# Moving the tiles of a matrix-product kernel to whole 2 KB addresses

## The chip, the cores and the metric

One core of a Trainium2 chip runs the kernel. The metric is the device time of one execution in microseconds. TensorE (PE) makes the matrix products, VectorE (DVE), ScalarE (ACT) and GpSimd (POOL) the rest; SyncE (SP) issues most DMAs. SBUF is the on-chip memory: 128 partitions, each a row of bytes, and an address here is a byte offset that is the same in all partitions. A tile of 128 rows by 512 fp32 elements takes 2048 bytes (2 KB) of every partition.

## The reference

One layer over 512 frames of width 2048: RMS norm, one input projection, two mixing branches (a gated recurrence and a differential attention), a projection of each branch, a gated merge, an output projection and the residual:

```python
h = rms_norm(x, norm_w[l])
proj = jnp.einsum('btd,dn->btn', h, w_in[l])
...
ya = hgrn2_mixer(a_q, a_f, a_i, lb_all[l], a_out_norm[l]).astype(x.dtype) * jax.nn.silu(a_g)
yb = diff_attention(b_q, b_k, b_v, b_q_norm[l], b_k_norm[l], b_lambda[l],
                    b_subln[l], lambda_init).astype(x.dtype) * jax.nn.silu(b_g)
ya = jnp.einsum('btw,wd->btd', ya, w_branch_a[l])
yb = jnp.einsum('btw,wd->btd', yb, w_branch_b[l])
mixed = jax.nn.sigmoid(gate_a) * ya + jax.nn.sigmoid(gate_b) * yb
x = x + jnp.einsum('btd,de->bte', mixed, w_out[l])
```

All of it is fp32. The kernel computes the large products with operands split in two float32r parts, a high and a low one, and three products of the parts (high by high, high by low, low by high).

## The kernel before

Nearly all the work is in `gemm` (line 148), which makes 512 columns of a projection. It goes over the contraction in blocks of 256 rows (`KC` = 2 times 128). For each block SP loads a `raw` tile (two rows of 512 elements, 4 KB, line 155), ACT rounds it to `whi` (line 167), DVE subtracts to get `wlo` (line 168), and PE makes 24 products: 4 output tiles by 2 contraction rows by 3 part pairs, all at line 183, all with a stationary operand of 128 by 128 elements (512 bytes of a partition, the slice `js` at 512 times j bytes into its tile) and a moving operand of 128 by 512 (2048 bytes). Every product loads its own stationary operand.

Three kinds of product stand at line 183, and the text names them by what moves:

- kind G: the normed input moves (`h_hi`, `h_lo`; tiles hh and hl), the weights (`whi`, `wlo`) are stationary. These are the first projections of branch A and the merge gates: 12 calls of 192 products, 2304 in all.
- kind W: the weights move, the normed input is stationary. These are the second projections of branch A (4 calls) and the projections of the 8 heads of branch B: 12 calls, 2304 products.
- kind S: the branch outputs or the merged rows move (tiles named s, from `split`), the weights are stationary. Branch projections (8 calls of 96) and the output projection (4 calls of 192): 1536 products.

The order of work is set by a scheduler that simulates the program; the code gives it priorities (`tc.high_priority`). The order in which `hybrid_block` calls things: branch A's four pairs of heads, each `proj_a` (a G call, then a W call) and two `mix_a`; the first two heads of branch B (`proj_b`, then `mix_b`); `merge` of branch A, in which G calls for the gates alternate with S calls; the other six heads of B; `merge` of branch B; the output projection. The small work of a mixer (products of 128 to 512 columns such as those of lines 294, 489 and 518, masks, exponentials) is interleaved with the products of the next call of `gemm`. I call a stretch of time in which that happens a mixer stage.

Where tiles lie is set by the pools (lines 69 to 73) in the order in which they are opened, each tile a multiple of 32 bytes. The first pool starts at address 16512, which is 128 past a whole 2 KB (16384). The pool `const` comes first, and in it the table `sm` (line 86, 292 elements, 1168 bytes), the small constants, then the 32 tiles of `h_hi` and `h_lo` (lines 107 and 108). In the built program the tiles lie, past the last whole 2 KB, at

| tiles | before | after |
|---|---|---|
| hh, hl (32 tiles of 2 KB) | 352 | 0 |
| raw (2), whi (3), wlo (3), 4 KB each | 1184 | 0 |
| slots s0 to s48 (2 KB each) | 1184 | 0 |
| qm (two of 3 KB, operand of line 294) | 288, 1312 | 0, 1024 |
| ident, the moving operand of the transposes | 1312 | 0 |

Since each large tile is a whole number of 2 KB long, all tiles of a row of this table have the same offset. A stationary slice adds 0, 512, 1024 or 1536 to it.

Of the kernel before, what the change touches and what calls it, by code (L numbers as in the profile page):

```python
# [10 lines left out]
F32 = mybir.dt.float32  # L11
F32R = mybir.dt.float32r
# [5 lines left out]
P = 128  # L18
T = 512
NT = T // P  # L20
D = 2048
NK = D // P
# [8 lines left out]
NSLOT = 49  # L31
PRIO = 3000
LEVELS = (2, 8, 32)


C_NW = 0
# [6 lines left out]
N_SMALL = C_LAM + 4 * QK  # L43
# [20 lines left out]
def hybrid_block(ctx: ExitStack, tc: tile.TileContext, xT, w_in, w_a, w_b, w_out,  # L64
# [1 line left out]
    nc = tc.nc  # L66
    MUL, ADD, SUB = ALU.mult, ALU.add, ALU.subtract

    const = ctx.enter_context(tc.tile_pool(name="const", bufs=1))
    wpool = ctx.enter_context(tc.tile_pool(name="wpool", bufs=3))  # L70
    spool = ctx.enter_context(tc.tile_pool(name="spool", bufs=1))
    small = ctx.enter_context(tc.tile_pool(name="small", bufs=4))
    qmp = ctx.enter_context(tc.tile_pool(name="qmp", bufs=2))
    ps_acc = ctx.enter_context(tc.tile_pool(name="ps_acc", bufs=4, space=bass.MemoryType.PSUM))
    ps_mix = ctx.enter_context(tc.tile_pool(name="ps_mix", bufs=4, space=bass.MemoryType.PSUM))

# [6 lines left out]
        return ps_mix.tile([P, T], F32, name="mix", tag="mix")  # L83


    sm = const.tile([P, N_SMALL], F32, name="sm")
    nc.scalar.dma_start(out=sm[:, 0:C_LAM], in_=smalls[:, 0:C_LAM])
    ident = const.tile([P, P], F32, name="ident")
    make_identity(nc, ident)
# [14 lines left out]
            slots.put(mi)  # L104


    h_hi = [const.tile([P, T], F32R, name=f"hh{k}") for k in range(NK)]
    h_lo = [const.tile([P, T], F32R, name=f"hl{k}") for k in range(NK)]
    xacc_s = slots.get()
    xacc = xacc_s[0]  # L110
    rstd_t = const.tile([P, NT], F32, name="rstd_t")
# [155 lines left out]
    def mix_a(head, q, sp, sn, vg, hh, dest):  # L267
# [19 lines left out]
        def scores(level, kt, qm):  # L287
            c = (1,) + LEVELS
            c = c[level]
            for half in range(2):  # L290
                ps = mix_tile()
                for i in range(2):
                    tt = half * 2 + i
                    nc.tensor.matmul(ps[:, i * 192:(i + 1) * 192], lhsT=kt[:, tt * P:(tt + 1) * P],  # L294
                                     rhs=qm[:, tt * 192:(tt + 1) * 192], start=True, stop=True)
                out = sc[:, half * 2:half * 2 + 2, :].rearrange("p i t -> p (i t)")
                mk = masks[:, level, :]
                if level == 0:
                    parts = ((0, 2, 0), (1, 2, 2))
                    w = 3  # L300
                    n = 2
                else:
                    parts = ((c, 4 * c, 0), (2 * c, 4 * c, 3 * c), (3 * c, 4 * c, 5 * c))
                    w = 6 * c
                    n = 4 * c
                ov = out.rearrange("p (g m) -> p g m", m=n)
                dv = ps[:, 0:384].rearrange("p (g m) -> p g m", m=w)
                kv = mk.rearrange("p (g m) -> p g m", m=w)
                for a, b, s0 in parts:
                    nc.vector.copy_predicated(out=ov[:, :, a:b], mask=kv[:, :, s0:s0 + b - a],  # L310
                                              data=dv[:, :, s0:s0 + b - a])
# [15 lines left out]

        for level, c in enumerate(LEVELS):
            G = T // (4 * c)
# [327 lines left out]
def _consts():  # L657
# [8 lines left out]
    for i in range(2):  # L666
        for g in range(P // 2):
# [3 lines left out]
            masks[:, 0, c0 + 2] = s == 2 * g  # L671
        for lv, c in enumerate(LEVELS):
            for g in range(P // (4 * c)):
# [46 lines left out]
```

## Time and profile before

| what | before |
|---|---|
| median of 3 runs | 1561.41 us (1559.88 to 1562.16) |
| the profiled execution's own time | 1564.39 us |
| its span, first to last instruction | 1562.6 us |
| mean granted TensorE clock | 0.997 of full speed |
| PE busy | 1546.7 us (99%) |
| DVE busy, ACT busy, POOL busy | 742.8 us (48%), 589.6 us (38%), 113.2 us (7%) |
| mean traffic | 100 GB/s |

The profiled execution is 3.0 us above the median and 1.8 us above its own span. A row of the chain of waits gives a start, a length and what ran: since the products follow each other without idle time, the length divided by the count is the step from the start of one product to the start of the next. The mean duration of one product in the tables is longer than this step, because products are pipelined and overlap; the step is what counts for the time.

### The profile page before, as it was taken

To read this page: it belongs to the slowest core of one execution; us is meant where nothing else is said; L and a number is where in the kernel's file an instruction comes from. 1 tells how busy PE (TensorE), PEld (TensorE's weight loads), DVE (VectorE), ACT (ScalarE), POOL (GpSimd) and SP (SyncE) were. 2 spreads that over 40 slices of the span, in tenths; PEclk is the share of its full clock that TensorE was granted. 3 is DMA by queue.
4 is the path that set the end of the run, shared out by engine and by line. 5 is a ranking of instruction groups with operands and counts; after the bars stand their busy time and mean duration, and the time that the engine had idled before them with its cause. 6 is when DMAs were issued, how large, how long until landed. Compare 5 with 4: busy or idle time off the path is not lost.

```text
span 1562.6 us, 18423 instructions
## 1 busy us (share of the span) xinstructions
PE 1546.7 (99%) x7096; PEld 1277.0 (82%) x7096; DVE 742.8 (48%) x1479; ACT 589.6 (38%) x866; POOL 113.2 (7%) x109
## 2 busy tenths in 40 slices
PE   7999999999999999999999999999999999999998
PEld 5888888888888888888888888888888888888887
DVE  8457656575674553322233454545453424442322
ACT  6533633544425552221213455445552222222111
POOL 7000000000011200000001011101100000000000
PEclk9999999999999999999999999999999999999999
DMA  6332222222323233333233333234323333354431
GB/s 213 95 108 68 75 89 77 87 80 68 96 81 97 79 104 92 95 94 96 95 94 102 108 102 100 83 101 103 103 78 94 95 96 95 94 161 148 148 122 68
DMA packets 149400, 155.50 MB, mean 100 GB/s; under 512 B 8192, under 2 KB 107392, under 8 KB 149312
## 3 DMA queue, kind: packets, MB, share of 16 engines
q1 hardware_dynamic: 142944, 143.55, 30.6%
q10 hardware_dynamic: 6288, 10.51, 2.5%
q8 instruction: 56, 0.92, 0.2%
q0 software_dynamic: 80, 0.26, 0.1%
q14 instruction: 32, 0.26, 0.0%
HBM read 143.80 MB, written 4.19 MB: 95 GB/s over the span
## 4 chain that ended last, share of the span: by engine, by line
PE 97%; DVE 1%; issue 1%; SPq 0%; DMA 0%; ACT 0%; DVEq 0%; ACTq 0%
PE acc L183 89%; PE mix L294 3%; PE mix L518 1%; DVE hl L119 1%; PE mix L490 1%; PE mix L489 1%; PE mix L511 1%; PE mix L379 0%; PE mix L453 0%; PE mix L254 0%; DVE wlo L168 0%; PE mix L368 0%; PE mix L382 0%; DMA raw<-in_w_in_dram 0%; SPq L406 0%
## 5 line engine op out<-in xcount | busy, mean ns | idle before, releaser
L168 DVE TENSOR_TENSOR wlo<-raw,whi 128x1024 fp32r<-128x1024 f32 (+1 forms) x257 | 317.2, 1234 | 620.0 <-ACT whi L167 604.1
L167 ACT ACTIVATE whi<-raw 128x1024 fp32r<-128x1024 f32 (+1 forms) x257 | 270.8, 1054 | 717.7 <-PE acc L183 634.8
L183 PE MATMUL acc<-s,whi 128*128 128x512 f32 x1024 | 313.3, 389 | 0.0
L183 PE MATMUL acc<-hh,whi 128*128 128x512 f32 x768 | 306.6, 400 | 5.9 <-ACT whi L167 5.9
L183 PE MATMUL acc<-hh,wlo 128*128 128x512 f32 x768 | 303.2, 400 | 6.0 <-DVE wlo L168 6.0
L183 PE MATMUL acc<-hl,whi 128*128 128x512 f32 x768 | 305.8, 399 | 0.0
L183 PE MATMUL acc<-whi,hh 128*128 128x512 f32 x768 | 303.9, 396 | 0.0
L183 PE MATMUL acc<-wlo,hh 128*128 128x512 f32 x768 | 303.4, 395 | 0.0
L183 PE MATMUL acc<-whi,hl 128*128 128x512 f32 x768 | 301.6, 395 | 0.0
L183 PEld LDWEIGHTS acc<-s,whi 128*128 128x128 f32 x1024 | 192.2, 188 | 40.2
L183 PE MATMUL acc<-s,wlo 128*128 128x512 f32 x512 | 197.1, 389 | 0.0
L183 PEld LDWEIGHTS acc<-hh,wlo 128*128 128x128 f32 x768 | 145.6, 190 | 41.6 <-DVE wlo L168 7.4
L183 PEld LDWEIGHTS acc<-hh,whi 128*128 128x128 f32 x768 | 145.2, 189 | 39.3 <-ACT whi L167 5.9
L183 PEld LDWEIGHTS acc<-hl,whi 128*128 128x128 f32 x768 | 145.2, 189 | 33.7
L183 PEld LDWEIGHTS acc<-whi,hl 128*128 128x128 f32 x768 | 144.5, 188 | 30.3
L183 PEld LDWEIGHTS acc<-wlo,hh 128*128 128x128 f32 x768 | 144.5, 188 | 30.2
L183 PEld LDWEIGHTS acc<-whi,hh 128*128 128x128 f32 x768 | 144.5, 188 | 29.2
L183 PEld LDWEIGHTS acc<-s,wlo 128*128 128x128 f32 x512 | 96.1, 188 | 19.9
L438 POOL TENSOR_TENSOR qr<-qs,mhalf 128x4 f32<-128x4 f32 x32 | 38.8, 1214 | 323.6 <-DVE qs L437 323.6
L310 DVE COPY_PREDICATED s<-s,mix 128x128 f32<-128x128 uint8 (+3 forms) x176 | 52.2, 339 | 14.7 <-PE mix L294 13.6
L294 PE MATMUL mix<-qm,s 128*128 128x192 f32 x256 | 46.9, 326 | 0.0
L495 ACT ACTIVATE s<-s,mn 128x128 f32<-128x128 f32 (+3 forms) x64 | 35.5, 556 | 26.9 <-DVE mn L492 26.9
(137 smaller groups left out, 1094.6 us busy)
## 6 DMA issues: line engine op xcount, KB each, us to landing
raw<-in_w_in_dram SPq DMA_DIRECT2D x240, 256.0 KB, 3.0
raw<-in_w_in_dram SPq DMA_DIRECT2D x64, 512.0 KB, 3.7
raw<-in_w_out_dram SPq DMA_DIRECT2D x32, 512.0 KB, 3.8
raw<-in_w_a_dram SPq DMA_DIRECT2D x16, 512.0 KB, 3.7
raw<-in_w_b_dram SPq DMA_DIRECT2D x16, 512.0 KB, 3.8
s<-s ACTq DMA_DIRECT2D x48, 128.0 KB, 3.9
s<-in_xT_dram SPq DMA_DIRECT2D x16, 256.0 KB, 4.2
raw<-in_w_in_dram SPq DMA_DIRECT2D x32, 128.0 KB, 2.9
```

The costliest lines, as they stand in the source:

```text
L119: nc.vector.scalar_tensor_tensor(out=h_lo[k], in0=x_t, scalar=nw, in1=h_hi[k].bitcast(F32), op0=MUL, op1=SUB)
L167: nc.scalar.activation(out=whi[:, cs, :], in_=raw[:, cs, :], func=AF.Copy)
L168: nc.vector.tensor_tensor(out=wlo[:, cs, :], in0=raw[:, cs, :], in1=whi[:, cs, :].bitcast(F32), op=SUB)
L183: nc.tensor.matmul(accs[j], lhsT=l, rhs=r, start=(k == 0 and n == 0), stop=(k == nk - 1 and n == 2))
L294: nc.tensor.matmul(ps[:, i * 192:(i + 1) * 192], lhsT=kt[:, tt * P:(tt + 1) * P], rhs=qm[:, tt * 192:(tt + 1) * 192], start=True, stop=True)
L310: nc.vector.copy_predicated(out=ov[:, :, a:b], mask=kv[:, :, s0:s0 + b - a], data=dv[:, :, s0:s0 + b - a])
L438: nc.gpsimd.tensor_tensor(out=rr, in0=ss, in1=mhalf[:, 0:4], op=ALU.pow)
L489: nc.tensor.matmul(pc, lhsT=q2[c][0][:, ts], rhs=k2[c][0][:, 0:nm], start=True, stop=False)
L490: nc.tensor.matmul(pc, lhsT=q2[c][0][:, ts], rhs=kl2[c][0][:, 0:nm], start=False, stop=True)
L495: nc.scalar.activation(out=pr[c][0][:, 0:n], in_=pr[c][0][:, 0:n], func=AF.Exp, scale=-1.0, bias=mn[:, e:e + 1], accum_out=z[:, e:e + 1])
L511: nc.tensor.transpose(pt[:, j * P:(j + 1) * P], w[:, j * P:(j + 1) * P], ident)
L518: nc.tensor.matmul(o[:, i * P:(i + 1) * P], lhsT=wTs[i][0][:, j * P:(j + 1) * P], rhs=tiles[j][0][:, 256:384], start=(j == 0), stop=(j == i))
```

## The change

The pools are opened in another order: a new pool `lead` that holds `sm` alone, widened from 292 to 480 elements (1920 bytes, so that 16512 and 1920 end at 18432, which is 9 times 2048), then a new pool `hpool` for `h_hi` and `h_lo`, then `wpool`, `spool` and `qmp`, and only then `const` and `small` with the small tiles. The widened part of `sm` is never written or read.

```diff
@@ -31,6 +31,7 @@
+LEAD = 480
@@ -66,11 +67,14 @@
-    const = ctx.enter_context(tc.tile_pool(name="const", bufs=1))
+
+    lead = ctx.enter_context(tc.tile_pool(name="lead", bufs=1))
+    hpool = ctx.enter_context(tc.tile_pool(name="hpool", bufs=1))
     wpool = ctx.enter_context(tc.tile_pool(name="wpool", bufs=3))
     spool = ctx.enter_context(tc.tile_pool(name="spool", bufs=1))
+    qmp = ctx.enter_context(tc.tile_pool(name="qmp", bufs=2))
+    const = ctx.enter_context(tc.tile_pool(name="const", bufs=1))
     small = ctx.enter_context(tc.tile_pool(name="small", bufs=4))
-    qmp = ctx.enter_context(tc.tile_pool(name="qmp", bufs=2))
@@ -83,7 +87,7 @@
-    sm = const.tile([P, N_SMALL], F32, name="sm")
+    sm = lead.tile([P, LEAD], F32, name="sm")
@@ -104,8 +108,8 @@
-    h_hi = [const.tile([P, T], F32R, name=f"hh{k}") for k in range(NK)]
-    h_lo = [const.tile([P, T], F32R, name=f"hl{k}") for k in range(NK)]
+    h_hi = [hpool.tile([P, T], F32R, name=f"hh{k}") for k in range(NK)]
+    h_lo = [hpool.tile([P, T], F32R, name=f"hl{k}") for k in range(NK)]
```

The score products with 128 rows, on top of which the change stands, are in both kernels (lines 481 to 490: two halves of 64 rows stacked). In the two built programs every engine and every queue has the same instructions in the same order with the same waits; only line numbers, the running numbers in tile names and the addresses differ.

## Rows read from the trace of the kernel before

**Rows 1.** The page: busy time by engine, and the chain that ended last.

```profile
PE 1546.7 (99%) x7096; PEld 1277.0 (82%) x7096; DVE 742.8 (48%) x1479; ACT 589.6 (38%) x866; POOL 113.2 (7%) x109
...
PE 97%; DVE 1%; issue 1%; SPq 0%; DMA 0%; ACT 0%; DVEq 0%; ACTq 0%
```

**Rows 2.** Waits, longest first: microseconds in total, times, longest; PE's are all of PE's.

```profile
PE acc L183 <- DVE wlo L168: 6.0, 3, 3.8
PE acc L183 <- ACT whi L167: 5.9, 1, 5.9
...
ACT whi L167 <- PE acc L183: 634.8, 179, 6.0
DVE wlo L168 <- ACT whi L167: 604.1, 191, 6.7
```

**Rows 3.** The page's groups at line 183: count, busy us, mean ns, idle before.

```profile
L183 PE MATMUL acc<-s,whi 128*128 128x512 f32 x1024 | 313.3, 389 | 0.0
L183 PE MATMUL acc<-hh,whi 128*128 128x512 f32 x768 | 306.6, 400 | 5.9 <-ACT whi L167 5.9
L183 PE MATMUL acc<-hh,wlo 128*128 128x512 f32 x768 | 303.2, 400 | 6.0 <-DVE wlo L168 6.0
L183 PE MATMUL acc<-hl,whi 128*128 128x512 f32 x768 | 305.8, 399 | 0.0
L183 PE MATMUL acc<-whi,hh 128*128 128x512 f32 x768 | 303.9, 396 | 0.0
L183 PE MATMUL acc<-wlo,hh 128*128 128x512 f32 x768 | 303.4, 395 | 0.0
L183 PE MATMUL acc<-whi,hl 128*128 128x512 f32 x768 | 301.6, 395 | 0.0
...
L183 PE MATMUL acc<-s,wlo 128*128 128x512 f32 x512 | 197.1, 389 | 0.0
```

**Rows 4.** Chain of waits, pieces: start us, length us, what, count; two gate calls (G).

```profile
655.92 44.10 PE acc L183 x189
...
721.81 44.33 PE acc L183 x190
```

**Rows 5.** Chain of waits: a branch projection and two output projections (S).

```profile
700.94 20.18 PE acc L183 x89
...
1384.96 42.16 PE acc L183 x186
...
1427.80 43.29 PE acc L183 x191
```

**Rows 6.** Chain of waits: the first W call, the second, and that of head 2.

```profile
64.98 44.10 PE acc L183 x189
...
173.94 40.53 PE acc L183 x177
...
810.83 43.26 PE acc L183 x189
```

**Rows 7.** PE by stretch: length, busy (count), granted clock, DMA share, GB/s.

```profile
655.30:700.10 44.80, 44.80 (x194) 1.00 0.31 94
...
1427.90:1471.40 43.50, 43.50 (x194) 1.00 0.46 146
...
64.40:109.20 44.80, 44.80 (x194) 1.00 0.30 94
...
6.00:39.00 33.00, 27.28 (x104) 0.99 0.67 217
```

**Rows 8.** Chain of waits: small products of branch A's mixer, line 294.

```profile
109.95 1.95 PE mix L294 x12
...
119.83 2.60 PE mix L294 x16
```

**Rows 9.** A mixer stage by engine: length, PE, PEld, DVE, ACT, POOL busy.

```profile
111.60:169.90 58.30, 58.30 (x293) 49.45 (x293) 39.98 (x106) 17.97 (x23) 3.61 (x5) 1.00 0.24 73
```

## The prediction

> **What bounds the kernel now.** I read the page first: PE is busy 99% of the span, and 97% of the chain that ended last is PE [rows 1]. Then the waits: PE waits for another engine only 11.9 us in all, four times [rows 2], while ACT waits 634.8 us for PE to give buffers back and DVE 604.1 us for ACT. So the preparation of the weights is far ahead, and the time is set by how fast PE starts one product after the other. A change that removes no instruction can then gain only if it shortens that step.
>
> So the third view is the chain of waits, cut into stages in which nothing but products of line 183 run. Length by count gives the step. Two gate calls (kind G, the normed input moves): 44.10 us for 189 and 44.33 for 190, 233.3 ns each [rows 4]. A branch projection and two output projections (kind S, slots move): 20.18 for 89, 42.16 for 186 and 43.29 for 191, 226.7 ns each [rows 5]. The products have the same shape, type, line and number of loads, and the granted clock is 1.00 (2.4 GHz) in both [rows 7]; DMA traffic is heavier in the faster one (146 against 94 GB/s). Means of one product say the same for all of them: 389 ns where s moves, 399 to 400 where hh or hl moves, 395 to 396 where the weights move [rows 3].
>
> What differs is where the operands lie. A stationary slice starts at a multiple of 512 bytes past its tile, so I compare offsets modulo 512. Kind S: moving 1184 is 160, stationary 1184 is 160, difference 0. Kind G: moving 352, stationary 160, difference 192. Kind W: moving 160, stationary 352, difference 320. The pair at equal offsets is the fast one in every stage. Within S the slots lie all over the upper half of the memory, and the step is the same: it is not the distance, it is the low part of the address.
>
> Kind W has two steps at the same addresses: 233.3 ns in the first call (44.10 for 189), 229.0 in the second (40.53 for 177) and 228.9 in the call for head 2 (43.26 for 189) [rows 6]. A fixed price for an unaligned start would give one value. So I read it as two streams of one engine, the moving operand and the load of the next stationary one, which run at the same time and get in each other's way, more or less so by their relative place and phase. The Trainium skill has a rule that speaks against this: in SBUF — State Buffer, Who interferes with whom, TensorE has two independent read ports, one for each operand, and never waits on anyone. By it an address could not change a step and the sum would be zero; the two steps above disagree with it, but no row shows which part of the memory is in conflict.
>
> **The change, part by part.**
>
> 1. The large tiles. After it every moving and stationary operand of line 183 lies at 0 modulo 512, difference 0, as kind S has now. The step of all three kinds then becomes 226.7 ns.
>    - G: 2304 products (three groups of 768) [rows 3]. The first 104 run in the start-up, where 27.28 us of PE work stand in 33.00 us [rows 7] and loads set the pace; I count nothing for them. 2200 times (233.3 - 226.7 = 6.68, unrounded) is 14.7 us.
>    - W: 192 products of the first call at 6.68 are 1.3 us; 2112 at 229.0 - 226.7 = 2.3 are 4.9 us. The W steps inside mixer stages I have not separated from the jumps between products; bounds for these 2112 are nothing and the full 6.68 (14.1 us). I take 2.3, the value of the two undisturbed calls.
>    - S: already at difference 0. 1536 products, nothing.
>
>    All of it lies on the path, since PE has no cover: sum 20.9 us.
> 2. `ident` and the qm tiles get other offsets. The products that read them are slower per column: 1.95 us for 12 and 2.60 for 16 products of 192 columns, 162.5 ns each [rows 8]. These pieces take in slices of both qm tiles, which start at eight different offsets, and both come to 162.5. Nothing.
> 3. The small tiles of `const` and `small` move to the end. They are read by DVE, ACT and POOL, whose operations also get new addresses for the large tiles. No row of before tells what an offset costs there; bounded by the busy shares (48% and 38%), it lies beside PE, and the cover is the 604 to 635 us that these engines wait [rows 2]. Nothing.
> 4. `raw` and the slots as targets of DMAs: loads land ahead of need after the start-up (no wait of PE for one in rows 2). In the start-up they could gain or lose a microsecond. Nothing.
> 5. Waits: none is added or removed, no queue is moved past another. What is late next if PE speeds up is the mixer's work: the stage at 111.6 has DVE busy 39.98 of 58.30 us [rows 9], and PE never waited there, so 1% less time should still fit. If that cover were gone it would be the second rival.
>
> Against the profiled execution's own time: 1564.4 - 20.9 = 1543.5 us. That execution stands 3.0 us above the median of the runs shown, so against the median the forecast is **1540.5 us**, 1.3% less.
>
> **The rivals.**
>
> - *Absolute alignment counts too, and every product gets faster.* A start at a whole 2 KB may save S something as well: now every moving operand crosses a 2 KB boundary inside its 2048 bytes, after the change none does. For it: S is still 226.7 ns, above the 213.3 ns that 512 columns take at one column per tick of the granted 2.4 GHz, and nothing in the trace explains the rest. Against it: three of the eight qm slices that line 294 moves cross such a boundary now, with no mark on the 162.5 ns of either piece [rows 8]. If each product goes down by one more difference of the size seen (6.68), 6144 of them give 41.0 us more: 1499.5 us. The Trainium skill has such a lower step: TensorE: Matmul & The Clock Gate, Back-to-back issue gap, gives N/2.4 + 2.5 ns, an estimate of 215.8 ns for 512 columns; by that the sum would be some 67 us more, and no row of before comes near it.
> - *The mixers set the pace.* PE is faster, but the stages with mixers keep their length, because DVE's chain was just in time. These hold 7 G calls (1344 products, 9.0 us) and 7 W calls (1344, 3.1 us); 8.8 us would stay: 1552.6 us. Against it: no wait of PE there in rows 2.
> - *Nothing changes.* Addresses do not matter and G differs from S for another reason, such as the region of the memory (hh and hl lie below the weights, s above). Then 1561.4. For it: the two W steps at the same addresses show that addresses alone don't fix the step. Against it: the step follows the kind in each of the undisturbed stages of G and S.
> - *The other pattern, slower.* All streams start at the same place modulo 512 and fall in the slower of the two patterns, as the first W call did and the later ones did not. The deciding point is the phase in which the first undisturbed product of a call starts. Then S goes from 226.7 to 233.3 (1536 times 6.68, 10.3 us) and W from 229.0 to 233.3 (2112 times 4.3, 9.1 us): 1580.8 us. Against it: S is at difference 0 now, is entered from G each time in the merges, and never shows 233.3.
>
> **How the numbers follow.** The forecast has 0.62, absolute alignment 0.12, mixers 0.08, nothing 0.10, the slower pattern 0.08. The range goes from 1531 (the forecast with the upper bound of W, 9.2 us more) up to 1564.5 (nothing changes, with 0.2% for the measurement); it holds the forecast, the mixers and no change, 0.80, and leaves out absolute alignment and the slower pattern. A measurement of this kernel can tell some 0.2% (3.1 us) from no change. Faster by more than that: 0.62 + 0.12 + 0.08 = 0.82; within: 0.10; slower: 0.08.
>
> **What would show it.** Right: in the gate calls some 190 products take 43.1 us instead of 44.1 to 44.3, the first W call the same, the later ones 228.9 to 226.7; S stays at 226.7; the means of all eight groups at line 183 come to 389 ns; waits of PE stay near 12 us. Absolute alignment: S falls below 226.7. Mixers: the undisturbed gate calls fall, but PE shows waits for DVE at lines 294, 489 or 518. Wrong: the gate calls keep 233.3, or S rises to it.

## The result, and the profile after

The changed kernel takes 1544.54 us (median of 4 runs, 1544.43 to 1545.92) against 1561.79 us for the kernel before (4 runs, 1559.88 to 1562.49): a ratio of 0.9894, 95% interval 0.9876 to 0.9911. That is 17.2 us less; 20.9 less was forecast, to 1540.5. The profiled execution took 1544.43 us with a span of 1542.6 us, the one of before 1564.39 with 1562.6: from trace to trace 20.0 us.

Busy times of the page, and all waits of PE (microseconds in total, times, longest):

```profile
PE 1527.6 (99%) x7096; PEld 1276.4 (83%) x7096; DVE 742.6 (48%) x1479; ACT 589.9 (38%) x866; POOL 113.1 (7%) x109
```

```profile
PE acc L187 <- ACT whi L171: 5.7, 1, 5.7
PE acc L187 <- DVE wlo L172: 5.3, 3, 2.9
```

No engine does less work than before [rows 1]: DVE, ACT and POOL are busy for the same time, PE's waits are 11.0 us for 11.9 [rows 2], and the mean granted clock is 0.998 of full speed for 0.997. PE alone is busy 19.1 us less, with the same 7096 products. Line 183 is now line 187. Five of the page's groups of it:

```profile
L187 PE MATMUL acc<-s,whi 128*128 128x512 f32 x1024 | 313.0, 389 | 0.0
L187 PE MATMUL acc<-hh,whi 128*128 128x512 f32 x768 | 302.7, 395 | 5.7 <-ACT whi L171 5.7
...
L187 PE MATMUL acc<-hl,whi 128*128 128x512 f32 x768 | 302.0, 394 | 0.0
...
L187 PE MATMUL acc<-whi,hh 128*128 128x512 f32 x768 | 301.6, 393 | 0.0
L187 PE MATMUL acc<-whi,hl 128*128 128x512 f32 x768 | 299.6, 392 | 0.0
```

Where hh and hl move, the mean fell from 399 to 400 ns to 394 to 395, and where the weights move from 395 to 396 ns to 392 to 393; where s moves it stayed [rows 3]. The pieces of the chain of waits (start, length, what, count) tell the steps of the undisturbed stages; in order of time the first W call, the second, a gate call (G), a branch projection (S), the W call of head 2 and an output projection (S). Here and below, the piece given for the first W call can begin with some products of the G call before it, which run at the same step:

```profile
59.80 38.31 PE acc L187 x169
...
169.22 40.15 PE acc L187 x177
...
644.79 42.39 PE acc L187 x187
...
689.00 20.17 PE acc L187 x89
...
797.79 41.25 PE acc L187 x182
...
1408.77 41.25 PE acc L187 x182
```

Length by count is 226.7, 226.8, 226.7, 226.6, 226.6 and 226.6 ns. Before, G took 233.3 [rows 4], S 226.7 [rows 5], and W 233.3 once and then 229 [rows 6]. All three kinds now have the step that S always had, and S has not moved.

### The profile page after: what moved, and what is told of

It is laid out like the page before. It is cut to its first block, busy times and chain, and to the rows that moved or that the text cites. A ratio compares the mean times of both kernels' runs of the same rounds, so it can differ in the third digit from the quotient of the medians.

```text
span 1542.6 us, 18423 instructions
## 1 busy us (share of the span) xinstructions
PE 1527.6 (99%) x7096; PEld 1276.4 (83%) x7096; DVE 742.6 (48%) x1479; ACT 589.9 (38%) x866; POOL 113.1 (7%) x109
## 4 chain that ended last, share of the span: by engine, by line
PE 97%; DVE 1%; DMA 1%; issue 0%; SPq 0%; ACT 0%; DVEq 0%
PE acc L187 89%; PE mix L298 3%; PE mix L522 1%; PE mix L494 1%; PE mix L493 1%; DVE hl L123 1%; PE mix L515 1%; PE mix L383 0%; PE mix L457 0%; PE mix L258 0%; DMA raw<-in_w_in_dram 0%; DVE wlo L172 0%; PE mix L372 0%; PE mix L386 0%; DMA s<-in_xT_dram 0%
## 5 line engine op out<-in xcount | busy, mean ns | idle before, releaser
L187 PE MATMUL acc<-hh,whi 128*128 128x512 f32 x768 | 302.7, 395 | 5.7 <-ACT whi L171 5.7
L187 PE MATMUL acc<-hh,wlo 128*128 128x512 f32 x768 | 298.8, 395 | 5.3 <-DVE wlo L172 5.3
L187 PE MATMUL acc<-hl,whi 128*128 128x512 f32 x768 | 302.0, 394 | 0.0
```

The source lines that it names most:

```text
L187: nc.tensor.matmul(accs[j], lhsT=l, rhs=r, start=(k == 0 and n == 0), stop=(k == nk - 1 and n == 2))
```

## The experiments

The theory: the step depends on the difference between the addresses of the moving and the stationary operand, in some low part of the address, and on nothing else of the layout. The rivals: the operand's own place (whole 2 KB, or the place 352) counts; the region of the memory or the place of the small tiles counts.

**1. The same difference, nothing at a whole 2 KB.** In the changed kernel:

```diff
-LEAD = 480
+LEAD = 568
```

> The changed kernel with all large tiles moved up together by 352 bytes: hh, hl, raw, whi, wlo and the slots all lie 352 past a whole 2 KB, so the difference between moving and stationary operand is a multiple of 512 as in the changed kernel, but no operand starts at a whole 2 KB and each moving operand crosses one. Theory, the difference counts: as the changed kernel, steps of 226.7 ns in every undisturbed stage, 1544.5 us within 1.5. Rival, the operand's own place counts (352 was the slow place of hh before): every moving operand of 6144 at 233.3, some 1544.5 + 41 = 1585 us; a milder form, a crossing of 2 KB costs: S above 226.7.

The kernel takes 1543.04 us (4 runs, 1542.66 to 1545.59); ratio to before 0.9879, interval 0.9864 to 0.9894, which overlaps that of the changed kernel. The chain of waits, in the first W call, a gate call, the W call of head 2 and an output projection:

```profile
59.99 38.08 PE acc L187 x168
...
643.86 42.16 PE acc L187 x186
...
796.86 41.25 PE acc L187 x182
...
1407.84 41.25 PE acc L187 x182
```

All four steps are 226.6 to 226.7 ns. With every large tile at 352, hh's old place, the whole gain is there. The rivals of the operand's own place fall, and with them the rival that a moving operand pays for crossing a 2 KB boundary: here each one crosses.

**2. The difference of before in the new layout.** In the changed kernel, a pool with one tile of 208 elements between `hpool` and `wpool`:

```diff
+    gap = ctx.enter_context(tc.tile_pool(name="gap", bufs=1))
     wpool = ctx.enter_context(tc.tile_pool(name="wpool", bufs=3))
...
+    fill = gap.tile([P, 208], F32, name="fill")
+    nc.vector.memset(fill, 0.0)
```

> The changed kernel with a gap of 832 bytes between the tiles of the normed input and all the others (and one small fill of the gap): hh and hl stay at whole 2 KB addresses, the weights and slots lie at 832, so the difference between them is that of the kernel before, 832 modulo 2048, with other absolute places. Theory, the difference counts: the kernel before, G at 233.3 ns, W at 229 to 233.3, S at 226.7, 1561.5 us within 3. Rival, the own place of the moving operand counts: G at 226.7 because hh lies as in the changed kernel, W and S where 832 puts them, below 1552 us if 832 is a good place. Rival, the order of the pools or the small tiles' new places count: 1544.5 us.

The kernel takes 1562.56 us (11 runs); ratio to before 1.0000, interval 0.9991 to 1.0009. The same four stages:

```profile
59.80 38.27 PE acc L190 x164
...
654.88 43.17 PE acc L190 x185
...
809.78 42.35 PE acc L190 x185
...
1427.79 41.25 PE acc L190 x182
```

233.4 ns in the first W call, 233.4 in the gate call, 228.9 in the W call of head 2, 226.6 in S: the kernel before, value for value, with hh and hl at whole 2 KB addresses and the pools and small tiles in the new order. The gain hangs on the difference; order of pools, small tiles and regions have no share in it beyond the 0.1% that the interval leaves.

**3. Eight differences in one kernel.** In the changed kernel (`LEAD` 352, so that the tiles fit), each second tile of hh and hl is longer:

```diff
-    h_hi = [hpool.tile([P, T], F32R, name=f"hh{k}") for k in range(NK)]
-    h_lo = [hpool.tile([P, T], F32R, name=f"hl{k}") for k in range(NK)]
+    def h_tile(name, k):
+        t = hpool.tile([P, T + k % 2 * STEP], F32R, name=f"{name}{k}")
+        return t[:, 0:T]
+
+    h_hi = [h_tile("hh", k) for k in range(NK)]
+    h_lo = [h_tile("hl", k) for k in range(NK)]
```

with `STEP` = 16 elements, 64 bytes.

> The changed kernel with 64 more bytes behind each second tile of hh and hl, so that the tiles of contraction block b (24 products of a call) lie b times 64 bytes past a multiple of 512, and all others at a multiple of 512: eight differences, 0 to 448, are measured in each call of kind G and W. Theory, the difference counts: a step that depends on the block, 226.7 ns at difference 0, 233.3 in G at 192, W at 229 to 233.3 in that block; S stays at 226.7 everywhere. If some difference gives less than 226.7, a faster kernel than both can be made. Rival, own place counts in whole 2 KB only: all blocks of G alike, at or above 233.3.

The kernel takes 1560.07 us (one run). The chain of waits in a gate call, 21 products of each of its eight blocks, at the differences 0, 64, 128, 192, 256, 320, 384 and 448; the second row is a part of the first block by itself:

```profile
652.58 4.80 PE acc L192 x21
...
655.34 3.40 PE acc L192 x15
...
658.06 4.81 PE acc L192 x21
...
663.57 4.88 PE acc L192 x21
...
669.14 4.90 PE acc L192 x21
...
674.73 4.78 PE acc L192 x21
...
680.20 4.82 PE acc L192 x21
...
685.71 4.88 PE acc L192 x21
...
691.30 4.90 PE acc L192 x21
```

In ns, for the eight blocks: 228.6, 229.0, 232.4, 233.3, and again 227.6, 229.5, 232.4, 233.3. The second half repeats the first, so what counts is the difference **modulo 256**. The first products of a block still feel the block before; the last 17 of the block at 256 take 226.7 each. The first block's 228.6 is a mixture: in the built program five products of the second block run among its first ones, and the 15 products behind them, all at difference 0, take 226.7. 192 is G of the kernel before and gives its 233.3; W of the kernel before is at 320, which is 64, and gives its 229. The expectation had W's 229 to 233.3 at 192 alone: there W takes 233.3, and its 229 belongs to 64. No difference gives less than 226.7.

**4. By 32 bytes.** `STEP` = 8 elements (and 64 elements behind the last hh tile, so that hl has the same offsets).

> As the scan by 64, with 32 bytes: differences 0 to 224. Theory, the difference counts, with a grain of 64 bytes: steps at 32 like those at 0 or 64, at 96 like 64 or 128; with a finer grain: values in between. At 0 226.7 ns, at 192 233.3 in G. S at 226.7.

The kernel takes 1566.83 us (one run). In a gate call at the differences 32, 96 and 160:

```profile
661.55 4.87 PE acc L192 x21
...
672.62 4.91 PE acc L192 x21
...
683.83 4.91 PE acc L192 x21
```

These are 231.9, 233.8 and 233.8 ns; the last 17 of the block at 32 take 233.4 each. So 32 is slow between 0 and 64, which are faster, and the guess of a grain of 64 bytes was wrong.

**5. By 4 bytes, near 0.** hh and hl are one tile each, and the blocks' slices begin 0, 4, 8, 16, 24, 240, 248 and 252 bytes past a multiple of 256:

```diff
+    SMALL = (0, 1, 2, 4, 6, 60, 62, 63)
+
+    def h_tiles(name):
+        big = hpool.tile([P, NK * T + 64], F32R, name=name)
+        return [big[:, k * T + SMALL[k // 2]:(k + 1) * T + SMALL[k // 2]] for k in range(NK)]
```

> The changed kernel with the tiles of the normed input of blocks 0 to 7 lying 0, 4, 8, 16, 24, 240, 248 and 252 bytes past a multiple of 256, all others at a multiple of 256 (hh and hl are one tile each, so that a few waits can stand elsewhere). It looks for a difference near 0 that is better than 0. Theory, streams that read the memory in pieces of 32 bytes or more: anything but 0 gives a step above 226.7 ns, most of them near the 233.4 ns that a difference of 32 showed in the scan by 32. Rival, a small lead of one stream gets it out of the other's way: some of 4 to 24 or 240 to 252 gives less than 226.7, and a version that beats both can be made.

The kernel takes 1563.32 us (one run). Moving minus stationary is 4 and 252 in two blocks of a gate call, and 16 and 4 in two blocks of the W call of head 2 (where h is stationary and lies at 240 and 252). The last row is the block at 4 of another W call, in a mixer stage, behind a break by small products:

```profile
660.03 4.03 PE acc L193 x17
...
692.79 4.80 PE acc L193 x21
...
835.98 4.79 PE acc L193 x21
...
847.05 4.76 PE acc L193 x21
...
951.40 3.73 PE acc L193 x16
```

These are 237.1, 228.6, 228.1, 226.7 and 233.1 ns. A difference of 4 bytes, a single element, costs G some 10 ns, here and in every G call but the one in the start-up. W takes 226.7 there in five calls, and some 233 in the other seven, where a mixer's small products break the stream. So below 32 bytes the difference is not all. Whether it matters which operand is off its place, or the order in which G and W take their operands, is not shown. "Anything but 0 gives a step above 226.7" has the five W calls as its one exception, and "most of them near the 233.4 ns" did not come: in the gate call the steps lie between some 228 and 237 ns. None goes below 226.7, so no version that beats difference 0 came out of the scans.

**6. What the time above one column per tick belongs to.** The kernel of experiment 3, in which all products but the first and last of a sum move 256 columns:

```diff
+                        first, last = k == 0 and n == 0, k == nk - 1 and n == 2
+                        w = T if first or last else T // 2
+                        nc.tensor.matmul(accs[j][:, 0:w], lhsT=l, rhs=r[:, 0:w], start=first, stop=last)
```

> The scan by 64 bytes with moving operands of 256 columns in place of 512 in all large products but the first and last of each sum; half of the columns of the large products are thus left out of the sum. It tells what the time above one column per tick belongs to. At difference 0 a product of 512 columns takes 544 ticks of 2.4 GHz (226.7 ns), 32 above its columns; at 192 it takes 560 (233.3), 48 above. Theory, the excess is the load of the next stationary operand (its 128 columns are read once per product, whatever moves): 288 ticks or 120.0 ns at difference 0, 304 ticks or 126.7 ns at 192. Rival, the excess is a loss per moving column: 272 ticks or 113.3 ns at 0, 280 or 116.7 ns at 192. If the loads of the weights or their preparation hold PE up, steps inside a block of 24 products still tell.

The kernel takes 1066.5 us (one run). The loads hold PE up in it, so only steps inside a block tell; the granted clock is 1.00 (2.4 GHz) in the stretches shown. The timeline of PE (start, length, what, count) in an output projection at difference 0, then at difference 192 in two G calls, a projection of branch A and a gate call, each with the first and the last of 19 products in a row:

```profile
981.73 0.28 PE L194 MATMUL acc<-s,wlo 128*128 128x256 f32 x1
981.85 0.40 PE L194 MATMUL acc<-s,whi 128*128 128x256 f32 x2
982.09 0.29 PE L194 MATMUL acc<-s,wlo 128*128 128x256 f32 x1
982.22 0.40 PE L194 MATMUL acc<-s,whi 128*128 128x256 f32 x2
982.45 0.28 PE L194 MATMUL acc<-s,wlo 128*128 128x256 f32 x1
```

```profile
247.39 0.28 PE L194 MATMUL acc<-hl,whi 128*128 128x256 f32 x1
...
249.43 0.28 PE L194 MATMUL acc<-hl,whi 128*128 128x256 f32 x1
...
470.38 0.28 PE L194 MATMUL acc<-hh,whi 128*128 128x256 f32 x1
...
472.50 0.28 PE L194 MATMUL acc<-hl,whi 128*128 128x256 f32 x1
```

From 981.73 to 982.45 are six steps, 120.0 ns each; from 470.38 to 472.50 eighteen, 117.8 each; from 247.39 to 249.43 eighteen, 113.3 each. At difference 0 the theory is met to the digit: 32 ticks above the columns, with 256 columns as with 512. At 192 it fails: 126.7 was due, and the blocks of G and W at 192 settle at one of two lasting steps, 117.8 or 113.3 ns, both below that at 0. The lower one is 272 ticks, 16 above its columns, so the 32 ticks are no fixed price for loading the next stationary operand; the rival's 116.7 did not come either. What the excess belongs to stays open. Which difference is good depends on how much moves, and the steps of experiment 3 hold for moving operands of 512 columns, which is all that this kernel's large products have.

**7. The kernel before, a second profile.**

> The kernel before, unchanged, for a second profile of it. Theory, at a difference other than 0 the step depends on the phase in which a call starts, so executions differ: the first W call, which showed 233.3 ns, or later ones, which showed 229, take other steps this time, and G stays at 233.3; the sum of the W steps differs from that of the first profile by up to 2 us. Rival, the program alone sets the pattern: every undisturbed call shows the step that it showed.

The kernel takes 1562.45 us (one run). The chain of waits, in the first and the second W call and a gate call:

```profile
64.00 34.07 PE acc L183 x146
...
172.03 40.53 PE acc L183 x177
...
653.77 43.40 PE acc L183 x186
```

The steps are 233.4, 229.0 and 233.3 ns, as in the first profile, call by call; the steps of all W products add up to 536.0 us in both. The rival is right: the program sets the pattern, not the chance of an execution. What differs between the two profiles is the first G call, in the start-up (56.8 against 55.2 us).

**8. 256 bytes instead of a new layout.** In the kernel before, pools in their old order:

```diff
+    const.tile([P, 16], F32, name="fill0")
     h_hi = [const.tile([P, T], F32R, name=f"hh{k}") for k in range(NK)]
...
+    const.tile([P, 48], F32, name="fill1")
```

> The kernel before, pools in their old order, with 64 unused bytes put ahead of hh and 192 behind the small tiles, so that hh and hl lie at 416 and the weights and slots at 1440 past a whole 2 KB: the difference is 1024, a multiple of 256, and nothing is at a whole 2 KB or in another order. Theory, the difference modulo 256 is all that counts: the time of the changed kernel, 1544.5 us within 2, all undisturbed steps 226.7 ns. Rival, whole 2 KB addresses or the place of the small tiles bring part of the gain: above 1548 us.

The kernel takes 1544.14 us (4 runs, 1543.21 to 1546.02); ratio to before 0.9888, interval 0.9871 to 0.9905. First W call, gate call, W call of head 2:

```profile
59.97 38.08 PE acc L184 x168
...
644.80 41.25 PE acc L184 x182
...
796.89 41.25 PE acc L184 x182
```

All three steps are 226.6 to 226.7 ns. The whole gain comes with two unused strips of 64 and 192 bytes; whole 2 KB addresses and the new order of the pools add nothing that can be measured.

**9. The first W call.** It kept 233.3 ns at the addresses at which the later undisturbed ones took 229. In the kernel before, four transposes more near its start:

```diff
+            def breaks():
+                mt = mix_tile()
+                for i in range(NT):
+                    nc.tensor.transpose(mt[:, i * P:(i + 1) * P], ident, ident)
+
+            later.append(breaks)
```

> The kernel before with four more transposes of the identity (128 columns each, into a tile that nobody reads) after the first block of the first W call, where the first W call of the kernel before runs unbroken out of a G stage and keeps 233.3 ns, while all others, at the same addresses, take 229. Theory, at a difference other than 0 the phase in which the two streams meet decides among several patterns, and a break resets it: after the break the first W call takes 229 ns. Rival, something else holds the first call at 233.3 (what the other engines do then, the loads): it keeps 233.3 on both sides of the break.

The kernel takes 1560.80 us (one run). The scheduler put them just ahead of the call's first product, not behind its first block, so both sides of the break can't be compared within the call; the call is compared with that of before [rows 6]:

```profile
61.32 0.44 PE mix L416 x4
61.76 43.97 PE acc L183 x192
```

That is 229.0 ns for all 192 products, for 233.3 without the break. At a difference of 64 the same addresses have two lasting patterns, and how the stream is entered picks one.

## Why the prediction was right

**What bounds the kernel** was right: PE's step is the time. No wait moved, and of the 20.0 us less span 19.1 are less PE busy time.

**The difference as the cause** was right, and is now shown both ways (experiments 1, 2 and 8). The forecast took the comparison modulo 512; it is modulo 256. The reading that the moving stream and the load of stationary operands get in each other's way fits experiment 1, where moving all operands together changes nothing, and the two patterns. It is argued and not shown: no run saw which part of the memory they share, and the excess per product is not simply the load of the next stationary operand (experiment 6). That stays open. The Trainium skill's rule (SBUF — State Buffer, Who interferes with whom: two independent read ports, TensorE waits on no one) does not describe this: 1 and 2 have the same tiles and instructions but for one fill, and differ by 19.5 us.

**The sum.** Added up over all products, the steps of G went from 555.0 to 540.4 us, of W from 536.0 to 530.9, of S from 348.1 to 347.9: 14.6, 5.1 and 0.2, together 19.9 against 20.9. That the two are so close is in part luck. Two terms differ from what came, and nearly cancel out:

- "The step of all three kinds then becomes 226.7 ns" holds in undisturbed stages alone. In mixer stages the first products after each small one are still irregular, and the mean of steps under 250 ns is 228.2, in five of the G calls (233.2 before) and 228.4 in the seven W calls (229.9 before). G's steps thus fell by 5.0 ns there, where 6.68 was counted. That took 1.6 us off G's term (960 products at 1.7 ns) and 1.1 us off W's (1344 at 0.8, since 1.5 came where 2.3 was taken).
- In the start-up call nothing was counted for 104 products and 0.6 us for the rest; it fell from 56.8 to 54.6 us. Experiment 7 has the unchanged kernel at 55.2 there, so 1.6 of these 2.2 us are the spread of the start-up and no effect of the change. With the steps of experiment 7 for the kernel before, the sum is 18.2 us: the forecast was 2.7 too large, and the step of the prediction that was mis-sized is the one above, on mixer stages.

**Trace and median.** The forecast of 1540.5 hung the sum on 1561.4, a median of three. The profiled execution of before was a long one of its kind (1564.39, where 15 later runs of that kernel lie between 1560.00 and 1564.52 with a median of 1562.59), that of after lies at the low end of four (1544.43 of 1544.43 to 1545.92, median 1544.54). Against 1562.59 the change gains 18.1 us. Of the 4.0 us between forecast and result, 2.7 are the sum, as experiment 7 shows it, and 1.2 the median of three (1561.41), which lies that much below 1562.59. Runs of one kernel spread over some 1.5 to 4.5 us.

**Parts 2 to 5** (ident and qm, small tiles, DMA targets, waits) were costed at nothing: experiment 2, which makes all these moves but for the difference, comes to before within 0.1%.

**The rivals.** Absolute alignment: S stayed at 226.7, and experiment 1 gives the gain without it. The 215.8 ns from the Trainium skill (TensorE: Matmul & The Clock Gate, Back-to-back issue gap, which gives its formula for an isolated product) was not reached at any difference; with 512 columns the lowest lasting step was 226.7. Mixers setting the pace: PE has no new wait, and the mixer stage of [rows 9] went from 58.3 to 57.3 us. Nothing changes: it does. The slower pattern: at difference 0 every undisturbed call takes 226.7, however it is entered; two patterns exist, but at other differences (64 in experiment 9, 4 in W in experiment 5).

**What would show it.** Gate calls, first and later W calls and S came out as written. "The means of all eight groups come to 389 ns" did not: 392 to 395 for G and W, since these means hold the start-up and the jumps of the mixer stages.

## What to carry to other kernels

When products of one shape take different steps at the same clock and nobody waits, compare the addresses of their two operands; a step from the chain of waits (length by count in an undisturbed stage) shows a few per cent that the busy share of 99% hides. Here it was enough that moving and stationary operands of 512 and 128 float32r columns had addresses equal modulo 256, which cost 256 bytes of padding and no other change. Measure the padding in one run by giving each contraction block its own offset, and do it for the width that the kernel uses; read the end of each block, since the scheduler can mix two of them. No run here tells of other types, or of a stationary operand that is kept for several products.

## What was not expected

- The grain is one element: a difference of 4 bytes took G from 226.7 to 237.1 ns, while W at the same difference stayed at 226.7 in five calls and took some 233 in seven.
- With 256 moving columns the order turns round: 120.0 ns at difference 0, and 117.8 or 113.3 at 192.
- At the difference 64 one program has two lasting patterns, 229.0 and 233.3 ns, which came back in the second profile, and four small products between two stages switch from one to the other.
